# One 512-column matmul for the weights' high part instead of two of 256, with half-bank sums added on the way out, in a split-precision layer stack

## The chip, the core and the metric

The kernel runs on one core of a Trainium2 chip. The metric is the device time of one execution in microseconds. A profiled execution has a span of its own, from its first to its last instruction; TensorE (PE) multiplies, with its weight loads (PEld) beside it, VectorE (DVE) and ScalarE (ACT) do the element-wise work and are the engines that read the matmuls' results, GpSimd (POOL) does small powers and some transfers, and SyncE's queue issues most transfers.

## The reference

`x` is one sequence of 256 tokens with 1024 features. Two blocks follow one another, each two layers deep. The first block's layer is attention and an MLP, the second's is a gated feed-forward network, a mixer and another such network:

```
def hybrid_layer(x, ...):
    proj = rmsnorm(x, n1) @ w_in                    # 1024 -> 2304: two kinds of heads
    ...                                             # rope, global GQA, dilated window attention
    x = x + y @ w_out
    u = jnp.square(jax.nn.relu(rmsnorm(x, n2) @ w_mlp_in))    # 1024 -> 4096
    return x + u @ w_mlp_out

def second_block(x, ...):
    for l in range(DEPTH):
        f = swiglu(x, ffn_w_gate[l, 0], ffn_w_up[l, 0], ffn_w_down[l, 0])   # 1024 -> 2816 -> 1024
        x = layer_norm(ALPHA * x + 0.5 * f, ...)
        z = x @ w_in[l]                             # three mixers: spatial gating, short convolution, RG-LRU
        ...
        x = layer_norm(ALPHA * x + y @ w_out[l], ...)
        f = swiglu(x, ffn_w_gate[l, 1], ffn_w_up[l, 1], ffn_w_down[l, 1])
        x = layer_norm(ALPHA * x + 0.5 * f, ...)
```

All inputs and weights are float32.

## The kernel before

Every large product is done in a split precision. A float32 operand becomes a high part (its fp32r rounding) and a low part (what is left), and a product is three matmuls (`mm3`): high by high, high by low, low by high. Weights come in **units** of 256 columns (`in_unit`) or 256 rows (`out_unit`) of a matrix. A unit is loaded by two 512 KB transfers into `wraw`, ACT casts the high part into `whi`, DVE subtracts for the low part into `wlo` (line 153); four units fit, so units are made ready ahead of their use. The activations, transposed, lie in `xT`: a high tile `xh` and a low tile `xl`, 8 groups of 128 features by 256 tokens.

Three forms of product use them. `a_form` gives 128 tokens by 256 columns, with `xh` and `xl` as the stationary operand and the weights moving: 8 groups of features by 3 matmuls of 256 columns, 24 in all. `b_form` gives a transposed result of 256 columns by 256 tokens: for each half `f` of the unit's columns the weights are stationary and the 256 tokens of `xh` or `xl` move, 24 matmuls of 256 columns each, 48 for a unit; both halves fill one PSUM bank, and one instruction of ACT or DVE takes the whole bank out (Relu at line 584, Silu at 679, a multiplication at 688, a copy at 733). `out_form` multiplies a hidden unit by the rows of the down projection, with 512 columns moving, 24 matmuls for a unit (`out_both`).

PSUM is in three pools: four banks `acc`, two `rot` and two `aux`. `a_form`, attention values and half of the `b_form`s use `rot`; transposes (through `aux()`), the gates of the mixer and the other `b_form`s use `aux`.

The steady part of a feed-forward network alternates gate `b_form`, `out_both` of an older unit, up `b_form`. Between stages stands `enter`: the last sums of the old stage go token half by token half (`finish`), `norm(t)` normalizes a half of 128 tokens and transposes it into the new `xT` by two banks of four transposes (line 227 or 262), and `fn(t, i)` are the first four `a_form`s of the new stage:

```
        if finish is not None:
            finish(0)
            finish(1, [0])
            norm(0)
            finish(1, [1])
        fn(0, 0)
        norm(1)
        fn(0, 1)
        fn(1, 0)
        fn(1, 1)
```

In attention, a string gives the order of the work, "p2 h1 h0 h2 sa0 sa1 p5 ta0 p7 ...": `p` is a projection (two `a_form`s), `h` the transposes of its two token halves (line 355; a key half waits for the scale `kss`, line 335), `sa` scores (line 364), `ta` transposes of the softmax weights (line 399). The order in which instructions stand on each engine is made from such program order by a scheduler that may pull an instruction ahead of earlier ones. Each engine then works through its own instructions in the order fixed there.

Of the kernel before, what the change touches and what calls it, by code (L numbers as in the profile page):

```python
# [12 lines left out]
F32R = mybir.dt.float32r  # L13
# [6 lines left out]
P = 128  # L20
# [3 lines left out]
KT = 8  # L24
# [21 lines left out]
def hybrid_stack(ctx: ExitStack, tc: tile.TileContext, a, out):  # L46
# [11 lines left out]
    tmp = ctx.enter_context(tc.tile_pool(name="tmp", bufs=2))  # L58
    tiny = ctx.enter_context(tc.tile_pool(name="tiny", bufs=2))
    accp = ctx.enter_context(tc.tile_pool(name="accp", bufs=4, space=PSUM))  # L60
    rotp = ctx.enter_context(tc.tile_pool(name="rotp", bufs=2, space=PSUM))
    auxp = ctx.enter_context(tc.tile_pool(name="auxp", bufs=2, space=PSUM))

    uid = [0]

# [4 lines left out]
    def T(pool, shape, tag, dt=F32, **kw):  # L70
        return pool.tile(shape, dt, tag=tag, name=nm(tag), **kw)
# [13 lines left out]
    def pair(shape):  # L85
        return T(tmp, shape, "pair", bufs=2)
# [5 lines left out]
        return T(rotp, list(shape), "rot")  # L92

    def aux(shape=(P, 512)):
        return T(auxp, list(shape), "aux")

    def acc1(shape=(P, 512)):
        return T(accp, list(shape), "acc")
# [2 lines left out]
        return [[acc1() for _ in range(2)] for _ in range(NT)]  # L101

    def new_xT():
        return padded(xtp, [P, KT, S], "xh", F32R), padded(xtp, [P, KT, S], "xl", F32R)

    def chunks():
        return [(c, slice(c * 512, (c + 1) * 512)) for c in range(2)]
# [65 lines left out]
            mm3(o[:, :UN], xT[0][:, k, ts], xT[1][:, k, ts], w[k][0], w[k][1], k == 0, k == KT - 1)  # L173
        return o[:, :UN]

    def b_form(xT, w, o, between=None):
        o = o.rearrange("p (f s) -> p f s", f=2)
        for f in range(2):
            if f and between:
                between()  # L180
            for k in range(KT):
                fs = slice(f * P, (f + 1) * P)
                mm3(o[:, f], w[k][0][:, fs], w[k][1][:, fs], xT[0][:, k], xT[1][:, k], k == 0, k == KT - 1)
        return o

    def out_form(acc, hT, k0, w, t, c, first, last):
        ts = slice(t * P, (t + 1) * P)
# [389 lines left out]
    def mlp(l, xT, boundary):  # L577
        n = FF1 // UN
        w1, w2 = a["w_mlp_in"][l], a["w_mlp_out"][l]

        acted = []

        def act(ps, r):
            acted[:] = [se.activation(r, ps, AF.Relu), ve.tensor_tensor(r, r, r, op=ALU.mult)]
            return r

        na = 2
        ws = [in_unit(w1, u) for u in range(na)]
        hidden = {}

        def start(t, u):
            hidden[u, t] = act(a_form(xT, ws[u], t, rot()), T(tmp, [P, UN], "qk", bufs=9))

        enter(boundary, start)
        hts = []

        def first_T():
            hts.extend(new_hT() for _ in range(na))
            hidden_T(hts, hidden)

        acc = None
        last = []
        for u in range(n):
            if u + na < n:
                h = act(b_form(xT, in_unit(w1, u + na), (rot, aux)[u % 2](), None if u else first_T), pair([P, 2, S]))
                hT = new_hT()
                split(hT, slice(None), h)
                hts.append(hT)
            if u == 0:
                acc = new_acc()  # L610
            if l == 0 and u == n // 2:
                with behind(acted):
                    prepare()
            w = out_unit(w2, u)
            if u < n - 2:
                out_both(acc, hts[u], 0, w, u == 0)
            else:
                last.append((hts[u], 0, w))
        return acc, out_last(acc, last)
# [31 lines left out]
    def ffn(l, i, xT, boundary):  # L651
# [24 lines left out]
        for u in range(n):  # L676
            if u + 1 < n:
                h = pair([P, 2, S])
                se.activation(h, b_form(xT, in_unit(wg, u + 1), rot(), None if u else first_T), AF.Silu)
            if u == 0:  # L680
                acc = new_acc()
            w = out_unit(wd, u)
            if u < n - 2:
                out_both(acc, hts[u], 0, w, u == 0)
            else:
                last.append((hts[u], 0, w))
            if u + 1 < n:
                ve.tensor_tensor(h, b_form(xT, in_unit(wu, u + 1), aux()), h, op=ALU.mult)
                hT = new_hT()
                split(hT, slice(None), h)  # L690
                hts.append(hT)
        return acc, out_last(acc, last)

    def mixers(l, xT, boundary):
# [34 lines left out]
        bx = T(m4k, [P, 4, S], "m4k")  # L729

        def recur_in(u, c0):
            ps = b_form(xT, in_unit(w_in, u), rot())
            se.copy(xrp[:, c0:c0 + 2, 3:], ps)
            for c in range(c0, c0 + 2):
                se.activation(xc[:, c], xrp[:, c, 0:S], AF.Identity, scale=rw[:, 4 * c:4 * c + 1], bias=rb[:, c:c + 1])
                for k in range(1, 4):
                    ve.scalar_tensor_tensor(xc[:, c], xrp[:, c, k:k + S], rw[:, 4 * c + k:4 * c + k + 1], xc[:, c],
                                            ALU.mult, ALU.add)
# [29 lines left out]
        def short_conv():  # L768
# [1 line left out]
            cg = six([P, 2, S])  # L770
            cup = T(tmp, [P, 2, S + 2], "cup", bufs=1)
            gp.memset(cup[:, :, 0:2], 0.0)
            se.copy(bg, b_form(xT, in_unit(w_in, 2), rot()))
            se.copy(cg, b_form(xT, in_unit(w_in, 3), rot()))
            ps = b_form(xT, in_unit(w_in, 4), rot())
            ve.tensor_tensor(cup[:, :, 2:], ps, cg, op=ALU.mult)
            y = six([P, 2, S])
            for c in range(2):
                ve.tensor_scalar(y[:, c], cup[:, c, 0:S], sw[:, 3 * c:3 * c + 1], None, ALU.mult)
# [12 lines left out]
        gg = []  # L792
        for i in range(2):
            g = six([P, 2, S])
            last = se.activation(g, b_form(xT, in_unit(w_in, 5 + i), rot()), AF.Gelu_apprx_tanh)
            gg.append(g)
            transpose_to(yT, 0, i, uu[i], 2)
        aa = T(m4k, [P, 4, S], "m4k")
# [155 lines left out]
```

## Time and profile before

| | |
|---|---|
| time, median of 3 runs | 1549.0 us (1548.07 to 1549.47) |
| profiled execution: time | 1550.74 us |
| profiled execution: span | 1549.0 us |
| mean granted TensorE clock | 0.995 |
| TensorE matmuls | 1513.0 us busy, 98% of the span, 10480 instructions |
| TensorE weight loads | 1393.5 us, 10480 instructions |
| VectorE | 1014.4 us, 65% |
| ScalarE | 816.8 us, 53% |
| transfers | 272.98 MB, 176 GB/s on average |

A row gives the time an engine was busy and that time's share of the span. Matmuls are pipelined and their ends are modelled, so that a matmul's own duration is longer than the distance from its start to the next one's; the distances between starts tell the rate.

### The profile page before, as it was taken

How to read it: one execution, taken by the hardware profiler on the slowest of the kernel's cores; microseconds unless marked ns; L12 is line 12 of the kernel's file. 1: busy time of each engine (PE TensorE's matmuls, PEld its weight loads, DVE VectorE, ACT ScalarE, POOL GpSimd, SP SyncE). 2: the span in 40 equal slices, each digit the busy share in tenths (PEclk: the TensorE clock that was granted, in tenths of full speed). 3: DMA queues.
4: the chain of work that ended last, by engine and by line, in shares of the span. 5: the costliest groups of instructions: out<-in, count | busy, mean ns of one | idle time of the engine just before them, and what ended most of it. 6: DMA issues, size and time to landing. Idle time of an engine off the chain costs nothing. (4 is left out here: it accounts for less than half of the span.)

```text
span 1549.0 us, 27008 instructions
## 1 busy us (share of the span) xinstructions
PE 1513.0 (98%) x10480; PEld 1393.5 (90%) x10480; DVE 1014.4 (65%) x2044; ACT 816.8 (53%) x1636; POOL 77.9 (5%) x118
## 2 busy tenths in 40 slices
PE   7999999989999999999999999999999999999998
PEld 7889989889899898999989899999999989899997
DVE  7977556579775555655577875556755477875554
ACT  7766544478574545544446554443644446554441
POOL 4000000040000000000011000000000010000000
PEclk9999999999999999999999999999999999999999
DMA  6525655544356654766646476664766647476661
GB/s 216 173 63 167 217 189 183 173 113 154 111 190 190 191 179 146 237 191 188 189 141 205 158 227 184 190 189 136 246 190 190 191 128 219 150 239 185 188 186 47
DMA packets 196368, 272.98 MB, mean 176 GB/s; under 512 B 9312, under 2 KB 169600, under 8 KB 196240
## 3 DMA queue, kind: packets, MB, share of 16 engines
q1 hardware_dynamic: 193664, 262.76, 55.1%
q0 software_dynamic: 2576, 8.50, 1.8%
q8 instruction: 82, 1.34, 0.4%
q14 instruction: 46, 0.38, 0.1%
HBM read 270.17 MB, written 1.05 MB: 175 GB/s over the span
## 5 line engine op out<-in xcount | busy, mean ns | idle before, releaser
L153 DVE TENSOR_TENSOR wlo<-wraw,whi 128x512 fp32r<-128x512 f32 x992 | 640.7, 686 | 365.7 <-ACT whi L153 356.8
L153 ACT CAST whi<-wraw 128x512 fp32r<-128x512 f32 x992 | 565.1, 619 | 527.1 <-issue 262.0
L166 PE MATMUL rot<-xh,whi 128*128 128x256 f32 x1088 | 307.0, 282 | 0.0
L167 PE MATMUL rot<-xl,whi 128*128 128x256 f32 x1088 | 305.9, 281 | 0.0
L168 PE MATMUL rot<-xh,wlo 128*128 128x256 f32 x1088 | 305.9, 281 | 0.0
L167 PE MATMUL aux<-xl,whi 128*128 128x256 f32 x864 | 242.5, 281 | 0.0
L166 PE MATMUL aux<-xh,whi 128*128 128x256 f32 x864 | 242.1, 280 | 0.0
L168 PE MATMUL aux<-xh,wlo 128*128 128x256 f32 x864 | 242.1, 280 | 0.0
L166 PE MATMUL acc<-whi,six 128*128 128x512 f32 x608 | 240.7, 396 | 0.1
L168 PE MATMUL acc<-whi,six 128*128 128x512 f32 x608 | 239.2, 395 | 0.2
L167 PE MATMUL acc<-wlo,six 128*128 128x512 f32 x608 | 238.8, 393 | 0.0
L167 PEld LDWEIGHTS rot<-xl,whi 128*128 128x128 f32 x1088 | 205.2, 189 | 0.6
L166 PEld LDWEIGHTS rot<-xh,whi 128*128 128x128 f32 x1088 | 205.1, 188 | 0.7
L168 PEld LDWEIGHTS rot<-xh,wlo 128*128 128x128 f32 x1088 | 205.0, 188 | 0.2
L167 PEld LDWEIGHTS aux<-xl,whi 128*128 128x128 f32 x864 | 162.5, 188 | 2.3
L166 PEld LDWEIGHTS aux<-xh,whi 128*128 128x128 f32 x864 | 162.5, 188 | 2.2
L168 PEld LDWEIGHTS aux<-xh,wlo 128*128 128x128 f32 x864 | 162.5, 188 | 0.0
L168 PE MATMUL rot<-whi,xl 128*128 128x256 f32 x544 | 155.6, 288 | 2.7 <-DVE xl L222 2.6
L166 PE MATMUL rot<-whi,xh 128*128 128x256 f32 x544 | 157.2, 290 | 0.5 <-ACT qk L705 0.5
L167 PE MATMUL rot<-wlo,xh 128*128 128x256 f32 x544 | 155.7, 286 | 0.2 <-DVE wlo L153 0.2
L168 PEld LDWEIGHTS acc<-whi,six 128*128 128x128 f32 x608 | 114.1, 188 | 28.5 <-DVE six L222 1.6
L166 PEld LDWEIGHTS acc<-whi,six 128*128 128x128 f32 x608 | 114.3, 188 | 24.3 <-ACT six L221 1.8
(217 smaller groups left out, 1731.6 us busy)
## 6 DMA issues: line engine op xcount, KB each, us to landing
wraw<-in_ffn_w_gate_dram SPq DMA_DIRECT2D x88, 512.0 KB, 4.5
wraw<-in_ffn_w_up_dram SPq DMA_DIRECT2D x88, 512.0 KB, 4.4
wraw<-in_ffn_w_down_dram SPq DMA_DIRECT2D x88, 512.0 KB, 4.3
wraw<-in_w_in_dram SPq DMA_DIRECT2D x71, 512.0 KB, 4.6
wraw<-in_w_mlp_in_dram SPq DMA_DIRECT2D x64, 512.0 KB, 4.3
wraw<-in_w_mlp_out_dram SPq DMA_DIRECT2D x64, 512.0 KB, 4.1
wraw<-in_w_out_dram SPq DMA_DIRECT2D x32, 512.0 KB, 4.0
g<-in_ln_g_dram POOLq DMA_DIRECT2D x6, 512.0 KB, 3.8
```

Source lines behind the costliest of these rows:

```text
L153: done[:] = [se.copy(h, r), ve.tensor_tensor(l, r, h.bitcast(F32), op=ALU.subtract)]
L166: pe.matmul(o, lh, rh, start=first, stop=False)
L167: pe.matmul(o, lh, rl, start=False, stop=False)
L168: pe.matmul(o, ll, rh, start=False, stop=last)
```

## The change

`xh` and `xl` become the two halves of one tile, `xT`, of 512 columns for each group of features. In `b_form` one matmul of 512 columns, with the weights' high part stationary, meets both; a second one of 256 columns, with the weights' low part, meets the high half and adds to the left half of the bank. Each half `f` of the unit so fills a bank of its own, whose two halves have to be added: ACT copies the right half to SBUF, DVE adds the left half to it and writes the result to `dst`. What used to read PSUM now reads that result. `rot` and `aux` become one pool of four banks.

```
-    rotp = ctx.enter_context(tc.tile_pool(name="rotp", bufs=2, space=PSUM))
-    auxp = ctx.enter_context(tc.tile_pool(name="auxp", bufs=2, space=PSUM))
+    rotp = ctx.enter_context(tc.tile_pool(name="rotp", bufs=4, space=PSUM))
...
     def aux(shape=(P, 512)):
-        return T(auxp, list(shape), "aux")
+        return T(rotp, list(shape), "rot")
...
     def new_xT():
-        return padded(xtp, [P, KT, S], "xh", F32R), padded(xtp, [P, KT, S], "xl", F32R)
+        x2 = padded(xtp, [P, KT, 2 * S], "xT", F32R)
+        return x2[:, :, :S], x2[:, :, S:], x2
...
-    def b_form(xT, w, o, between=None):
-        o = o.rearrange("p (f s) -> p f s", f=2)
+    def b_form(xT, w, dst, between=None):
+        x2 = xT[2]
         for f in range(2):
             if f and between:
                 between()
+            fs = slice(f * P, (f + 1) * P)
+            o = rot()
             for k in range(KT):
-                fs = slice(f * P, (f + 1) * P)
-                mm3(o[:, f], w[k][0][:, fs], w[k][1][:, fs], xT[0][:, k], xT[1][:, k], k == 0, k == KT - 1)
-        return o
+                hi = lambda **kw: pe.matmul(o, w[k][0][:, fs], x2[:, k], **kw)
+                lo = lambda **kw: pe.matmul(o[:, :S], w[k][1][:, fs], x2[:, k, :S], **kw)
+                if k < KT - 1:
+                    hi(start=k == 0, stop=False)
+                    lo(start=False, stop=False)
+                else:
+                    lo(start=False, stop=False)
+                    hi(start=False, stop=True)
+            tb = T(tmp, [P, S], "ti", bufs=2)
+            se.copy(tb, o[:, S:])
+            ve.tensor_tensor(dst[:, f], o[:, :S], tb, op=ALU.add)
...
+        def square(r):
+            acted[:] = [ve.scalar_tensor_tensor(r, r, 0.0, r, ALU.max, ALU.mult)]
...
-                h = act(b_form(xT, in_unit(w1, u + na), (rot, aux)[u % 2](), None if u else first_T), pair([P, 2, S]))
+                h = pair([P, 2, S])
+                b_form(xT, in_unit(w1, u + na), h, None if u else first_T)
+                square(h)
...
-                se.activation(h, b_form(xT, in_unit(wg, u + 1), rot(), None if u else first_T), AF.Silu)
+                b_form(xT, in_unit(wg, u + 1), h, None if u else first_T)
+                se.activation(h, h, AF.Silu)
...
-                ve.tensor_tensor(h, b_form(xT, in_unit(wu, u + 1), aux()), h, op=ALU.mult)
+                up = four([P, 2, S])
+                b_form(xT, in_unit(wu, u + 1), up)
+                ve.tensor_tensor(h, up, h, op=ALU.mult)
...
-            ps = b_form(xT, in_unit(w_in, u), rot())
-            se.copy(xrp[:, c0:c0 + 2, 3:], ps)
+            b_form(xT, in_unit(w_in, u), xrp[:, c0:c0 + 2, 3:])
```

The other `b_form`s of the mixer change in the same way. Beyond these lines the change moves instructions that it does not touch, on PE at three places. The lines of the changed kernel are 12 to 20 higher than those of before (355 is 367 there, 364 is 376, 227 is 239, 743 is 762, 763 is 782).

The first is PE in attention of the first layer, behind projection p2. Before, the transposes of heads h1, h0 and h2 (line 355) stand between matmuls of projection p5 (`rot_605`):

```order
L355 MATMUL aux_525<-ident_99,qk_335 128x128 x2
L355 MATMUL aux_529<-ident_99,qk_413 128x128 x2
L166 MATMUL rot_605<-whi_590,xh_109 128x256
L167 MATMUL rot_605<-wlo_591,xh_109 128x256
L355 MATMUL aux_533<-ident_99,qk_260 128x128 x2
L168 MATMUL rot_605<-whi_590,xl_110 128x256
L355 MATMUL aux_537<-ident_99,qk_374 128x128 x2
L166 MATMUL rot_605<-whi_590,xh_109 128x256
...
L355 MATMUL aux_541<-ident_99,qk_477 128x128 x2
```

After `aux_541` (the first half of h2) 30 further matmuls of p5 stand ahead of the second half of h2, then 6 more and the scores. In the changed kernel all six stand together, ahead of p5 (`rot_600`), of which four matmuls stand ahead of the scores (line 376) and 44 behind them:

```order
L367 MATMUL rot_520<-ident_96,qk_330 128x128 x2
L367 MATMUL rot_524<-ident_96,qk_408 128x128 x2
L367 MATMUL rot_528<-ident_96,qk_255 128x128 x2
L367 MATMUL rot_532<-ident_96,qk_369 128x128 x2
L367 MATMUL rot_536<-ident_96,qk_472 128x128 x2
L367 MATMUL rot_540<-ident_96,qk_517 128x128 x2
L166 MATMUL rot_600<-whi_585,xT_106 128x256
L167 MATMUL rot_600<-wlo_586,xT_106 128x256
L168 MATMUL rot_600<-whi_585,xT_106 128x256
L166 MATMUL rot_600<-whi_585,xT_106 128x256
L376 MATMUL acc_544<-m4k_111,m4k_110 128x256
```

So p5 moved from between the transposes to behind the scores. The same holds in the second layer.

The second place is PE at `enter` in the second block, here from the first mixer to its feed-forward network. Before, the second token half's transposes (`x_7357`) stand behind the whole `a_form` of `fn(0, 0)`, 24 matmuls, and behind 19 of the 24 of `fn(0, 1)` (`rot_12405`):

```order
L227 MATMUL aux_12322<-ident_99,x_7291 128x128 x4
L227 MATMUL aux_12331<-ident_99,x_7291 128x128 x4
...
L166 MATMUL rot_12405<-whi_12267,xh_12240 128x256
L227 MATMUL aux_12389<-ident_99,x_7357 128x128 x4
L167 MATMUL rot_12405<-wlo_12268,xh_12240 128x256
L227 MATMUL aux_12398<-ident_99,x_7357 128x128 x4
L168 MATMUL rot_12405<-whi_12267,xl_12241 128x256
```

In the changed kernel (here from a network to the next) they stand ahead of all of `fn(0, 1)`, which is `rot_11704`:

```order
L239 MATMUL rot_11621<-ident_96,x_7001 128x128 x4
L239 MATMUL rot_11630<-ident_96,x_7001 128x128 x4
...
L168 MATMUL rot_11650<-whi_11550,xT_11540 128x256
L239 MATMUL rot_11688<-ident_96,x_7067 128x128 x4
L239 MATMUL rot_11697<-ident_96,x_7067 128x128 x4
L166 MATMUL rot_11704<-whi_11558,xT_11540 128x256
L167 MATMUL rot_11704<-wlo_11559,xT_11540 128x256
```

So 19 matmuls moved from ahead of these transposes to behind them. This is so at five boundaries: two into a mixer, two out of one, one between two networks. The other boundaries have the same order in both kernels.

The third is PE in the mixer, behind the sums of spatial gating (line 763). Before, the four gates (line 743) stand among the first 21 matmuls of the next `b_form` (`rot_9734`):

```order
L763 MATMUL aux_9662<-qk_9347,four_9491 128x64 x4
L763 MATMUL aux_9680<-qk_9429,four_9491 128x64 x4
L166 MATMUL rot_9734<-xh_9237,whi_9719 128x256
...
L743 MATMUL aux_9689<-m4k_9502,m4k_9496 128x256 x2
L168 MATMUL rot_9734<-xh_9237,wlo_9720 128x256
```

In the changed kernel the four stand together ahead of it:

```order
L782 MATMUL rot_9180<-qk_8886,four_9029 128x64 x4
L782 MATMUL rot_9198<-qk_8968,four_9029 128x64 x4
L762 MATMUL rot_9207<-m4k_9040,m4k_9034 128x256 x2
L762 MATMUL rot_9214<-m4k_9040,m4k_9034 128x256 x2
L762 MATMUL rot_9221<-m4k_9040,m4k_9034 128x256 x2
L762 MATMUL rot_9228<-m4k_9040,m4k_9034 128x256 x2
L186 MATMUL rot_9252<-xT_8777,whi_9237 128x512
```

So 21 matmuls moved behind the gates, in both layers.

## Rows read from the trace of the kernel before

**Rows 1.** The page: busy time of each engine, share of the span, instructions.
```profile
PE 1513.0 (98%) x10480; PEld 1393.5 (90%) x10480; DVE 1014.4 (65%) x2044; ACT 816.8 (53%) x1636; POOL 77.9 (5%) x118
```
**Rows 2.** Groups of TensorE: line, tiles, shape, count | busy us, mean ns | idle before.
```profile
L166 PE MATMUL rot<-xh,whi 128*128 128x256 f32 x1088 | 307.0, 282 | 0.0
...
L166 PE MATMUL aux<-xh,whi 128*128 128x256 f32 x864 | 242.1, 280 | 0.0
```
**Rows 3.** Timeline of PE in a feed-forward network: start us, duration us, operation.
```profile
666.20 0.39 PE L166 MATMUL acc<-whi,six 128*128 128x512 f32 x1
...
671.70 0.28 PE L166 MATMUL aux<-xh,whi 128*128 128x256 f32 x1
...
683.01 0.39 PE L166 MATMUL acc<-whi,six 128*128 128x512 f32 x1
...
688.56 0.28 PE L166 MATMUL aux<-xh,whi 128*128 128x256 f32 x1
```
**Rows 4.** Window of nearly nine feed-forward iterations: busy time (count) of PE, PEld, DVE, ACT.
```profile
640.00:790.00 150.00, 150.00 (x1090) 141.67 (x1089) 79.27 (x126) 70.00 (x126) 0.00 (x0) 1.00 0.64 192
```
**Rows 5.** Groups of ACT and of DVE that read a bank, or half of one.
```profile
L356 ACT COPY m4k<-aux 128x256 f32<-128x256 f32 x28 | 9.5, 375 | 6.1 <-PE aux L355 6.1
L584 ACT ACTIVATE pair<-rot 128x512 f32<-128x512 f32 x14 | 8.3, 595 | 0.0
L663 DVE TENSOR_TENSOR qk<-rot,qk 128x256 f32<-128x256 f32 x8 | 3.4, 419 | 0.3 <-PE rot L168 0.3
```
**Rows 6.** Timeline of PE in attention, first layer, with idle time and releaser.
```profile
40.75 0.41 PE L355 MATMUL aux<-ident,qk 128*128 128x128 f32 x2 [1.46 <-DVE qk L335]
...
41.79 2.00 PE L364 MATMUL acc<-m4k,m4k 64*128 64x256 f32 x16
...
49.77 0.44 PE L399 MATMUL aux<-ident,six 128*128 128x128 f32 x2 [2.12 <-DVE six L397]
```
**Rows 7.** The same, second layer.
```profile
340.76 0.41 PE L355 MATMUL aux<-ident,qk 128*128 128x128 f32 x2 [0.91 <-DVE qk L335]
...
348.83 0.44 PE L399 MATMUL aux<-ident,six 128*128 128x128 f32 x2 [1.15 <-DVE six L397]
```
**Rows 8.** Windows there; behind the five engines stands the granted clock.
```profile
336.00:338.00 2.00, 2.00 (x10) 2.00 (x11) 2.00 (x8) 1.34 (x4) 1.02 (x1) 0.50 0.24 19
338.00:341.00 3.00, 2.09 (x15) 1.92 (x14) 1.63 (x5) 1.06 (x3) 1.91 (x3) 0.83 0.74 218
```
**Rows 9.** Timeline at the first boundary out of a mixer: PE, then DVE.
```profile
887.48 1.25 PE L227 MATMUL aux<-ident,x 128*128 128x128 f32 x8
895.14 0.63 PE L227 MATMUL aux<-ident,x 128*128 128x128 f32 x4
...
889.38 1.28 DVE L222 TENSOR_TENSOR xl<-aux,xh 128x512 fp32r<-128x512 f32 x2
...
891.18 0.67 DVE L290 SCALAR_TENSOR_TENSOR x<-acc,x 128x512 f32<-128x512 f32 x1
894.25 1.41 DVE L299 SCALAR_TENSOR_TENSOR x<-x,lms,b 128x512 f32<-128x512 f32 x2
```
**Rows 10.** Timeline of PE at the first boundary into a mixer.
```profile
809.76 0.38 PE L166 MATMUL rot<-whi,xh 128*128 128x256 f32 x1 [0.26 <-ACT qk L705]
...
811.56 0.39 PE L168 MATMUL rot<-whi,xl 128*128 128x256 f32 x1 [1.30 <-DVE xl L222]
```
**Rows 11.** Timeline of PE at the gates, first and second mixer.
```profile
828.18 1.89 PE L763 MATMUL aux<-qk,four 128*128 128x64 f32 x16
...
839.86 0.47 PE L166 MATMUL rot<-xh,whi 128*128 128x256 f32 x1
...
1295.29 1.89 PE L763 MATMUL aux<-qk,four 128*128 128x64 f32 x16
1301.55 1.89 PE L743 MATMUL aux<-m4k,m4k 128*128 128x256 f32 x8
1303.09 0.47 PE L166 MATMUL rot<-xh,whi 128*128 128x256 f32 x1
```

More of the change, by code (lines that the diff above doesn't have):

```diff
@@ L772, in short_conv @@
             gp.memset(cup[:, :, 0:2], 0.0)
[L773 to L776, printed above, removed]
+            b_form(xT, in_unit(w_in, 2), bg)
+            b_form(xT, in_unit(w_in, 3), cg)
+            b_form(xT, in_unit(w_in, 4), cup[:, :, 2:])
+            ve.tensor_tensor(cup[:, :, 2:], cup[:, :, 2:], cg, op=ALU.mult)
             y = six([P, 2, S])
@@ L794, in mixers @@
             g = six([P, 2, S])
-            last = se.activation(g, b_form(xT, in_unit(w_in, 5 + i), rot()), AF.Gelu_apprx_tanh)
+            b_form(xT, in_unit(w_in, 5 + i), g)
+            last = se.activation(g, g, AF.Gelu_apprx_tanh)
             gg.append(g)
```

## The prediction

> **What bounds the kernel now.** I read the page first: matmuls are busy for 98% of the span, DVE for 65%, ACT for 53% [rows 1]. So the question is where TensorE (PE) stands still, and what a matmul costs it. The groups show that `b_form`'s matmuls have no idle time before them [rows 2]: where they run, PE alone sets the pace. Its idle time lies at a few places that the timeline shows: attention, where transposes wait for DVE [rows 6, 7], the boundary into a mixer [rows 10] and the gates [rows 11]. The windows show that in a steady feed-forward stretch DVE works 79 and ACT 70 of 150 us [rows 4]: they wait for PE, not PE for them. The change can therefore gain only by making PE's own stream shorter, and lose by making PE wait where it does not wait now.
>
> **The steps of the matmuls.** `b_form` has 1088 + 864 = 1952 groups of three matmuls [rows 2]. From 671.70 to 683.01 there are two `b_form`s, 96 matmuls of 256 columns: 11.31 / 96 = 117.8 ns from start to start. From 683.01 to 688.56 stand 24 matmuls of 512 columns: 5.55 / 24 = 231.3 ns; from 666.20 to 671.70 another 24 take 5.50, 229.2 ns [rows 3]. A group costs 3 x 117.8 = 353.4 ns before, and 231.3 + 117.8 = 349.1 after, if the new 512-column matmul, whose moving operand is the activation, runs like these, whose moving operand is the weight. That is 4.3 ns for each group, **-8 us** in all (1952 x 4.3 ns = 8.4). The bounds are the columns alone (768 before and after: no gain, 0 us) and the shorter stretch (6.4 ns, -12 us). So nearly all that PE streams stays; the third weight load that goes lay beside a matmul.
>
> The Trainium skill (TensorE: Matmul & The Clock Gate, Back-to-back issue gap) gives the distance of matmuls at the full clock as the columns at 2.4 GHz plus 2.5 ns. By it each group saves 2.5 ns, 4.9 us in all, and the sum below would end 3 us higher; but it would also make the steps 109 and 216 ns, where this trace shows 118 and 231 [rows 3], so the rows decide.
>
> **The way out.** Each of the 122 `b_form`s (1952 / 16) gets two ACT copies and two DVE additions of 128x256. The nearest rows are 375 ns for an ACT copy out of a bank and 419 ns for a DVE operation with one operand in PSUM [rows 5]: 244 x 0.375 = 92 us on ACT, 244 x 0.419 = 102 us on DVE. Against this the MLP's 28 Relus of 595 ns go from ACT [rows 5]; its squares stay one DVE instruction, and Silu and the product read SBUF instead of PSUM. In 150 us stand about 8.9 iterations of 16.8 us, with 4 of each: DVE goes from 79 to about 94 us, ACT from 70 to about 83 [rows 4]. The cover is PE's own work: a hidden unit is used only after another `b_form` of 5.65 us [rows 3], and the added chain is below 1 us. I take 0. With that cover gone it would be 122 x 0.8 = 98 us, if each wait stood open on PE.
>
> **Attention.** Here p5 moves behind the scores. In the first layer the second half of head h2 is transposed at 40.75, released by DVE, after PE had idled 1.46 us; the chain of `kss` through DVE and POOL keeps its place in both orders, so this time stays [rows 6]. Before, PE has run 42 matmuls of p5 by then and spends the stretch from the scores (41.79, 2.00 us) to the first `ta0` transposes (49.77) on 31 of p7 and 2.12 us of waiting [rows 6]. After, it waits without cover ahead of 40.75, and then has p5's 44 matmuls, 44 x 0.118 = 5.2 us, for the same gap; they end near 49. At 49.77 PE has saved at most 0.9 us of `ta0` against 31 x 0.118 = 3.7 us of p7 not yet done: 2.8 us late. In the second layer 16 matmuls of p7 stand ahead of `ta0` at 348.83 [rows 7]: 16 x 0.118 = 1.9 us late. Nothing behind it gives this back, for PE has little idle time there.
>
> The clock adds to it. In the second layer, after PE had waited, the granted clock was 0.50 from 336 to 338 and still 0.83 on average to 341 [rows 8]: half of 2.4 GHz for 2 us and, at 0.83 of a mean, for (1 - 0.83) x 2 x 3 = 1.0 us more, 3 us at the least. Before, part of that spell lay where PE waited anyway. After, PE has hardly any work for 8 us ahead of the scores in both layers, and the spell falls on p5 and the scores: 3 / 2 = 1.5 us each. The bounds are 0 and twice that. Attention: 2.8 + 1.9 + 2 x 1.5 = **+7.7 us**.
>
> **Boundaries.** At 887.48 the first token half is transposed, at 895.14 the second, 7.66 us later [rows 9]. What lies between on DVE is a chain that the change leaves in its order: `xl` at 889.38, statistics, the sum at 891.18, the last normalization from 894.25, and the transposes stand right behind it [rows 9]. PE filled this with 8 transposes, 6 matmuls of 512 and 43 of 256 columns. Now 19 of the 43 stand behind the transposes, so PE comes 19 x 0.118 = 2.2 us early and waits; behind the transposes they cover nothing, since PE does not wait there now. Three boundaries (two out of a mixer, one between networks): 3 x 2.2 = 6.6 us. At the two into a mixer PE waits behind the transposes now, 0.26 + 1.30 us [rows 10], and the 19 matmuls cover that: 2 x (2.2 - 1.6) = 1.2 us. **+7.8 us.** The bounds are 0, if DVE's chain came 2.2 us sooner, and 11. A fall of the clock behind each wait (1.5 us, five times) is left to the range.
>
> **Gates.** From the gating sums to the end of the gates and 21 matmuls PE takes 11.68 us in the first mixer and 7.80 in the second, of which 1.89 + 4 x 0.77 + 21 x 0.118 = 7.45 is work (two gates from 1301.55 to 1303.09) [rows 11]. The gates wait for DVE and ACT in the first. With the 21 matmuls behind them, up to 2.5 us of cover goes; against that each half of a projection's channels now leaves PSUM 2.8 us before the other, which brings the inputs sooner. The bounds are 0 and 5; I take **+1 us**.
>
> **Sum:** -8 + 7.7 + 7.8 + 1 = +8.5 us. Against the profiled execution, 1550.7 us with a span of 1549.0, that gives 1559.2; its time lies 1.7 us above the median, so the median goes from 1549.0 to 1557.5, **1558 us**.
>
> **Rivals.**
> 1. *About even, 1549 us.* The waits are shorter than the matmuls that left them, because DVE or ACT reach the chains sooner with four shared banks: half of attention and of the boundaries, 8 instead of 15.5, cancels the 8 us. For it: a bank no longer waits for its one partner. Against it: the chains end in DVE and POOL [rows 6, 9], which no bank holds up.
> 2. *Faster, 1541 us.* The saving of 8 us comes alone. The mechanism is the place of PE's late releases: DVE's normalization of the second half would have to end 2.2 us sooner than at 895, and the `kss` chain some 3 us sooner than at 40.75; from half of that on it gains. The rows show both chains busy without gaps that the change could take out.
> 3. *Slower by more, 1565 us.* The clock falls at each of the five boundaries, 5 x 1.5 = 7.5 us. For it: it fell behind waits of this length in attention [rows 8]. Against it: the mean granted clock of the whole span is 0.995, so of PE's many waits few end in a fall.
> 4. *Evacuation binds, above 1580 us.* The additions hold up DVE's subtractions for the weights, which stand behind them in its queue, and PE waits for `wlo`. It decides where DVE has under 15 us of 150 to spare; it has 70 [rows 4].
>
> **How the numbers follow.** My case has 0.64 and its own range is 1552 to 1565; rival 1 has 0.15, rival 2 0.10, rival 3 0.08, rival 4 0.03. The runs of before lie within 0.1% of each other, so 0.2%, 3.1 us, is about what a measurement can tell from no change. Slower by more than that: my case but for its lowest edge, and rivals 3 and 4, 0.74. Within it: rival 1 and that edge, 0.16. Faster: 0.10. The range takes in the upper half of rival 1 and rival 3 up to its time: 1547 to 1566.
>
> **What would show it.** In the changed profile the matmuls and weight loads should be 8528 each (10480 - 1952); 512-column steps in `b_form` of 229 to 235 ns and 256-column ones near 118; PE idle for 3 to 5 us ahead of each key head's second half, with the clock at 0.5 behind it; a wait of about 2 us released by DVE ahead of the second transposes at five boundaries; DVE near 1115 us and ACT near 890, without PE waiting for either in the networks. I am wrong if `b_form` groups fall below 340 ns, if DVE's chain ends sooner at the boundaries, or if PE waits inside the networks.

## The result, and the profile after

The changed kernel takes 1570.0 us (median of 4 runs, 1567.6 to 1572.4) against 1548.5 beside it: a ratio of 1.0137, 95% interval 1.0122 to 1.0152. It is slower, as forecast, but by 21.5 us where 8.5 were worked out, and 4 us above the range. The profiled execution has a span of 1570.6 us.

The page of the changed kernel, the line of [rows 1], and two of its groups, which answer to [rows 2]:

```profile
PE 1514.8 (96%) x8528; PEld 1305.4 (83%) x8528; DVE 1113.9 (71%) x2288; ACT 879.3 (56%) x1844; POOL 79.0 (5%) x118
L186 PE MATMUL rot<-xT,whi 128*128 128x512 f32 x1952 | 681.8, 396 | 0.0
L187 PE MATMUL rot<-xT,wlo 128*128 128x256 f32 x1952 | 507.1, 280 | 0.0
```

The counts came as worked out (8528), the two engines' busy times nearly so (1115 and 890 us were given), and nothing stands idle ahead of a `b_form`. So what the loss is made of lies elsewhere, and a table by stage says where. A stage is counted from its first normalized transposes (line 262 or 227, 274 or 239 after) to those of the next, as the timelines show them; the last ends with the last matmul.

| stage | before, us | after | difference |
|---|---|---|---|
| attention, first layer | 121.40 | 128.68 | +7.28 |
| MLP | 182.03 | 181.83 | -0.20 |
| attention, second layer | 118.22 | 122.03 | +3.81 |
| MLP | 182.92 | 182.18 | -0.74 |
| network | 190.94 | 191.17 | +0.23 |
| mixer | 87.67 | 86.99 | -0.68 |
| network | 189.07 | 192.45 | +3.37 |
| network | 188.88 | 192.84 | +3.96 |
| mixer | 85.05 | 88.83 | +3.78 |
| network | 190.84 | 192.02 | +1.18 |

With -0.34 us at the start that is +21.65. Attention has half of it, although it holds no `b_form` at all. These are stages of one profiled execution of each kernel; how much the first one varies while its order stays is said further below.

**Steps of the matmuls.** The timeline of the changed kernel where two `b_form`s follow one another, as in [rows 3]:

```profile
664.35 0.40 PE L186 MATMUL rot<-xT,whi 128*128 128x512 f32 x1
...
675.63 0.40 PE L166 MATMUL acc<-whi,six 128*128 128x512 f32 x1
```

675.63 - 664.35 = 11.28 us for 32 groups, against 11.31 in [rows 3]. Over the 34 such pairs of each trace the mean went from 11.325 to 11.246 us: 2.5 ns a group, 4.8 us in all instead of 8.4. The new 512-column matmul stands 233.6 ns ahead of the next start (the mean over the trace, without steps over 270 ns), not 231.3. By the gap formula of the Trainium skill (TensorE: Matmul & The Clock Gate, Back-to-back issue gap), which the page gives for an isolated matmul, the saving is estimated at 2.5 ns a group, as measured, though the formula's steps of 109 and 216 ns stand in neither trace.

**Attention.** TensorE in the first layer after the change, to be read beside [rows 6], and the windows of the half-speed stretches in both layers (behind the five engines stands the granted clock):

```profile
36.95 0.66 PE L367 MATMUL rot<-ident,qk 128*128 128x128 f32 x2 [4.53 <-DVE qk L347]
42.35 0.66 PE L367 MATMUL rot<-ident,qk 128*128 128x128 f32 x2 [4.74 <-DVE qk L347]
43.80 2.98 PE L376 MATMUL acc<-m4k,m4k 64*128 64x256 f32 x16
52.09 1.03 PE L411 MATMUL rot<-ident,six 128*128 128x128 f32 x8
```
```profile
38.00:46.00 8.00, 3.65 (x18) 3.08 (x20) 6.63 (x18) 4.74 (x10) 2.94 (x3) 0.51 0.70 192
343.00:353.00 10.00, 5.83 (x25) 4.09 (x24) 7.34 (x20) 5.40 (x11) 2.93 (x3) 0.50 0.66 198
```

TensorE waits ahead of both halves of the key head, 4.5 and 4.7 us. Before, the second of these waits was 1.46 [rows 6], and the first:

```profile
35.35 0.41 PE L355 MATMUL aux<-ident,qk 128*128 128x128 f32 x2 [1.68 <-DVE qk L335]
```

The clock goes to half for 10.24 us in each layer, and for 3.41 us at 103.9 in the first, where the kernel before has one such fall, 3.41 us long, in the second; the scores take 2.98 instead of 2.00 us; and the `ta0` transposes come 2.3 us later than in [rows 6], at 52.09, when all of p5 but none of p7 is done.

**Boundaries.** At the first boundary out of a mixer, which [rows 9] show for before: TensorE, then DVE and ACT ahead of it.

```profile
896.83 1.29 PE L239 MATMUL rot<-ident,x 128*128 128x128 f32 x8 [1.97 <-DVE x L311]
904.53 1.29 PE L239 MATMUL rot<-ident,x 128*128 128x128 f32 x8 [2.14 <-DVE x L311]
...
888.10 1.29 DVE L153 TENSOR_TENSOR wlo<-wraw,whi 128x512 fp32r<-128x512 f32 x2 [0.84 <-ACT whi L153]
890.33 1.29 DVE L153 TENSOR_TENSOR wlo<-wraw,whi 128x512 fp32r<-128x512 f32 x2 [0.93 <-ACT whi L153]
891.54 0.68 DVE L302 SCALAR_TENSOR_TENSOR x<-acc,x 128x512 f32<-128x512 f32 x1
...
889.67 1.15 ACT L153 CAST whi<-wraw 128x512 fp32r<-128x512 f32 x2 [1.09 <-DMA wraw<-in_ffn_w_up_dram]
```

The wait ahead of the second transposes is the 2.2 us that was forecast. The one ahead of the first, 1.97 us here and as long behind the second mixer, was not: DVE comes to the sum `x<-acc` only when it has done ten subtractions for the next network's weights, and the last two wait for a cast of ACT, which waits for a transfer. Before, seven subtractions stand directly ahead of the same sum, and it waits for its matmuls alone:

```profile
880.75 0.69 DVE L290 SCALAR_TENSOR_TENSOR x<-acc,x 128x512 f32<-128x512 f32 x1 [0.31 <-PE acc L168]
```

**Gates.** From the gating sums to the end of the gates and 21 matmuls' worth of `b_form` (7 groups of 0.35 us), the stretch of [rows 11]:

```profile
839.57 1.89 PE L782 MATMUL rot<-qk,four 128*128 128x64 f32 x16
...
845.53 0.59 PE L186 MATMUL rot<-xT,whi 128*128 128x512 f32 x1
...
1310.69 1.89 PE L782 MATMUL rot<-qk,four 128*128 128x64 f32 x16
...
1319.52 0.58 PE L186 MATMUL rot<-xT,whi 128*128 128x512 f32 x1
```

845.53 + 2.46 - 839.57 = 8.4 us in the first mixer, 11.3 in the second, against 11.68 and 7.80: -3.3 in the one and +3.5 in the other, +0.2 us in all.

### The profile page after: what moved, and what is told of

Read it like the earlier page. It is cut to its first block, busy times and chain, and to the rows that moved or that the text cites. A ratio compares the mean times of both kernels' runs of the same rounds, so it can differ in the third digit from the quotient of the medians.

```text
span 1570.6 us, 23644 instructions
## 1 busy us (share of the span) xinstructions
PE 1514.8 (96%) x8528; PEld 1305.4 (83%) x8528; DVE 1113.9 (71%) x2288; ACT 879.3 (56%) x1844; POOL 79.0 (5%) x118
## 5 line engine op out<-in xcount | busy, mean ns | idle before, releaser
L186 PE MATMUL rot<-xT,whi 128*128 128x512 f32 x1952 | 681.8, 396 | 0.0
L187 PE MATMUL rot<-xT,wlo 128*128 128x256 f32 x1952 | 507.1, 280 | 0.0
L186 PEld LDWEIGHTS rot<-xT,whi 128*128 128x128 f32 x1952 | 355.4, 188 | 68.9
L187 PEld LDWEIGHTS rot<-xT,wlo 128*128 128x128 f32 x1952 | 367.2, 188 | 21.5
L195 ACT COPY ti<-rot 128x256 f32<-128x256 f32 x244 | 90.9, 372 | 162.0 <-PE rot L186 162.0
L166 PE MATMUL rot<-whi,xT 128*128 128x256 f32 x544 | 158.4, 292 | 2.8 <-ACT whi L153 2.8
L168 PE MATMUL rot<-whi,xT 128*128 128x256 f32 x544 | 155.8, 287 | 1.6 <-DVE xT L234 1.6
L167 PE MATMUL rot<-wlo,xT 128*128 128x256 f32 x544 | 156.5, 288 | 0.1
L167 PEld LDWEIGHTS acc<-wlo,six 128*128 128x128 f32 x608 | 114.1, 188 | 26.2
L166 PEld LDWEIGHTS rot<-whi,xT 128*128 128x128 f32 x544 | 106.5, 196 | 3.9 <-ACT whi L153 3.2
L167 PEld LDWEIGHTS rot<-wlo,xT 128*128 128x128 f32 x544 | 106.4, 195 | 2.3 <-issue 1.0
L168 PEld LDWEIGHTS rot<-whi,xT 128*128 128x128 f32 x544 | 105.8, 195 | 2.2 <-DVE xT L234 2.2
```

The source lines that it names most:

```text
L166: pe.matmul(o, lh, rh, start=first, stop=False)
L167: pe.matmul(o, lh, rl, start=False, stop=False)
L168: pe.matmul(o, ll, rh, start=False, stop=last)
L186: hi = lambda **kw: pe.matmul(o, w[k][0][:, fs], x2[:, k], **kw)
L187: lo = lambda **kw: pe.matmul(o[:, :S], w[k][1][:, fs], x2[:, k, :S], **kw)
L195: se.copy(tb, o[:, S:])
```

## The experiments

The theory after the result was that nothing but the order costs time, and that the order comes from the common pool: a tile of a pool is not given out ahead of one that was asked for earlier, so with one pool p5's bank stands behind the head's banks in line. The orders below agree with that rule of giving out banks; no run tests the rule by itself. Two edits that the change makes together were therefore taken apart.

**One pool alone.** In the kernel before:

```
-    rotp = ... tile_pool(name="rotp", bufs=2, space=PSUM)
-    auxp = ... tile_pool(name="auxp", bufs=2, space=PSUM)
+    rotp = ... tile_pool(name="rotp", bufs=4, space=PSUM)
```

> The kernel before, with its rot and aux banks in one pool of four and nothing else changed; its instructions stand in the order of the changed kernel in attention, at the boundaries and at the gates. Theory A (the common pool's order is the loss, the matmul form is a gain of 5.3 us): 1548.5 + 21.5 + 5.3 = 1575 us, with PE waiting 4 to 5 us at each key head and 2.2 us ahead of the second transposes. Theory B (the additions on the way out delay DVE's chains at the boundaries, 4.4 us of the loss in the trace): 1571 us, without the 2.1 us waits ahead of the first transposes out of a mixer. Theory C (the 512-column form itself is the loss): 1549 us.

1571.9 us, ratio 1.0146 (1.0132 to 1.0159): the pool alone costs as much as the whole change. Its stages of attention take 128.52 and 121.68 us, as in the changed kernel. Theory C is out. At the boundary out of the first mixer:

```profile
895.93 1.29 PE L226 MATMUL rot<-ident,x 128*128 128x128 f32 x8
903.64 1.29 PE L226 MATMUL rot<-ident,x 128*128 128x128 f32 x8 [2.15 <-DVE x L298]
```

There is a wait ahead of the second transposes, none ahead of the first, so that one needs the new `b_form` as well, as theory B has it.

**Two pools, a half of each `b_form` in either.** In the changed kernel, the pools of before, and:

```
-            o = rot()
+            o = (rot, aux)[f]()
```

> The changed kernel with two pools of two banks again; half 0 of each b_form takes a rot bank, half 1 an aux bank. The order of before comes back. Theory A: the saving of the steps alone, 1548.5 - 5.3 = 1543 us. Theory B: 1548 us, since the additions stay in DVE's queue ahead of the normalizations. Theory C: 1570 us as the changed kernel.

1560.1 us, ratio 1.0073 (1.0060 to 1.0085): none of the three. Attention came back to 123.42 and 120.22 us, but each MLP and network has a new wait in its first `b_form`:

```profile
148.63 0.51 PE L167 MATMUL acc<-whi,six 128*128 128x512 f32 x1 [1.12 <-ACT six L234]
```

The second half takes an aux bank, the hidden unit's transposes hold aux banks, and so the order put matmuls of `out_both` between the halves, which wait for those transposes. Six such waits are 7.2 us; the 8.3 us named further below count short ones in the mixers too. The run also keeps the waits ahead of the first transposes (2.07 and 1.94 us), with ten subtractions ahead of the sum in DVE's queue as in the changed kernel.

**p5 ahead of h2 in the string**, one pool:

```
-    "p2 h1 h0 h2 sa0 sa1 p5 ta0 p7 ...
+    "p2 h1 h0 p5 h2 sa0 sa1 ta0 p7 ...
```

> The changed kernel with its one pool, and projection p5 ahead of head h2 in the string of attention, which is all that changes. Theory A (PE idles at the key heads because no matmuls are left to stand there, and the clock falls behind that): both layers get back what they lost, 7.3 + 3.8 = 11 us, 1559 us. Rival (only the waits come back, the wait moves behind the scores and the clock falls all the same): 1566 us. Rival (the chain of kss sets the pace wherever p5 stands): 1570 us.

1574.6 us, ratio 1.0170 (1.0154 to 1.0186), outside all three. The timeline of the second layer:

```profile
345.53 3.78 PE L376 MATMUL acc<-m4k,m4k 64*128 64x256 f32 x16 [0.65 <-ACT m4k L368]
354.11 3.17 PE L376 MATMUL acc<-m4k,m4k 64*128 64x256 f32 x8 [4.79 <-ACT six L395]
```

With p5 gone from there, the third scores were pulled up behind the second, where they wait 4.79 us for a softmax to give back a bank of `acc`. In the first layer the two waits at the key head did shrink to one of 2.36 us, and the layer took 125.20 us for 128.68; the second took 129.54 for 122.03. A string in this kernel is a wish, and its place on TensorE has to be read afterwards; the time of this run says nothing for or against the theory.

**Second transposes behind all of fn(0, 1)**, one pool, at every boundary:

```
         fn(0, 0)
-        norm(1)
         fn(0, 1)
+        norm(1)
```

> The changed kernel with its one pool, and at every boundary the second token half's normalization and transposes behind all of fn(0, 1), 24 matmuls of 256 columns. Theory A (the transposes stand 2.3 us too early in PE's queue at five boundaries and the clock falls behind two of them): 5 x 2.3 + 3.4 less 1 to 4 us of new waits behind the transposes, 1558 to 1560 us. Theory B (DVE's chain ends late because of the additions, whatever stands on PE): PE waits for the products that follow instead, 1567 us.

1564.5 us, ratio 1.0098 (1.0084 to 1.0111), 5.5 us less than the changed kernel, between the two. At the boundary of the rows above:

```profile
902.91 1.03 PE L239 MATMUL rot<-ident,x 128*128 128x128 f32 x8
904.18 0.38 PE L166 MATMUL rot<-whi,xT 128*128 128x256 f32 x1 [0.24 <-ACT xT L233]
905.33 0.38 PE L168 MATMUL rot<-whi,xT 128*128 128x256 f32 x1 [0.42 <-DVE xT L234]
```

The wait ahead of the second transposes is gone, and 0.66 us came back behind them, where nothing covers ACT's and DVE's work on what was transposed. At the two boundaries into a mixer it is 1.8 and 1.9 us, more than the theory had allowed.

**Two pools, both halves in rot.** The changed kernel with the pools of before and nothing else:

> Two pools of two banks again, and both halves of every b_form take rot banks; the order on PE is that of before nearly everywhere. Theory D (in the run with halves in both pools, 8.3 us were waits of the first b_form of a stage for an aux bank that its transposes held; what is left is 4 us of waiting ahead of the first transposes behind the two mixers, some 3.5 us of clock falls, and -5.3 us of steps): 1560.1 - 8.3 = 1552 us. Rival, the additions are not hidden at the start of a stage, whatever bank they read: 1560 us. Theory A as it stood: 1543 us.

1545.9 us, ratio 0.9986 (0.9977 to 0.9995): this version beats both kernels, by 0.14% and 1.5%. It is between theories A and D; the 4 us ahead of the first transposes that D kept are not there. Its DVE, at the end of the first mixer:

```profile
876.63 4.90 DVE L154 TENSOR_TENSOR wlo<-wraw,whi 128x512 fp32r<-128x512 f32 x8
881.45 0.68 DVE L303 SCALAR_TENSOR_TENSOR x<-acc,x 128x512 f32<-128x512 f32 x1
```

Eight subtractions stand ahead of the sum, not ten. The additions of the mixer are all still there, so they do not bring the wait by themselves, as theory B had it. The wait goes with how far the weights' work was pulled ahead in DVE's queue: seven subtractions directly ahead of the sum in the kernel before and with the pool alone, eight here, and no such wait; ten in the changed kernel and in the run with a half in either pool, and a wait behind both mixers.

**The same, with the mixers' b_forms as before** (three matmuls, one read of the bank, at the seven units of a mixer):

> As the run with two pools and all halves in rot, but the mixers' b_forms are again three matmuls of 256 columns with one read of the bank; networks and MLP keep the 512-column form. Theory D (the mixer's additions on DVE wait for PE and hold up the weights' subtractions behind them, so that the normalization at the mixer's end starts late): the 4 us ahead of the first transposes go, 14 x 16 x 2.7 ns = 0.6 us of steps come back, 1548.5 us. Rival, the normalization is late because the weights' transfers are late: 1552 us, with the waits still there.

1546.8 us, ratio 0.9988 (0.9979 to 0.9997), no different from the run above. With nothing waiting there any more, the run could not tell its theories apart; what it shows is that the new form costs the mixers nothing that can be measured.

**The way out twice**, one pool:

```
+            for _ in range(2 if twice else 1):
-            se.copy(tb, o[:, S:])
-            ve.tensor_tensor(dst[:, f], o[:, :S], tb, op=ALU.add)
+                se.copy(tb, o[:, S:])
+                ve.tensor_tensor(dst[:, f], o[:, :S], tb, op=ALU.add)
```

> The changed kernel with one pool, and in the networks and the MLP each copy of ACT and each addition of DVE on the way out is done twice (108 b_forms, 216 copies and 216 additions more: 80 us more on ACT, 91 on DVE). If the way out lies beside PE's work there: 1570 us as the changed kernel, within 3 us. Rival, it stands on the path at the start and the end of each stage (12 places by 2 x 0.8 us): 1580 us or more. If it stood open everywhere: 1656 us.

1571.1 us, ratio 1.0143 (1.0129 to 1.0157), 1.1 us above the changed kernel and within its runs. The windows of a steady stretch, the changed kernel and this one (PE, PEld, DVE, ACT):

```profile
640.00:790.00 150.00, 149.98 (x785) 127.31 (x784) 95.95 (x166) 84.67 (x168) 0.54 (x1) 1.00 0.65 198
```
```profile
640.00:790.00 150.00, 150.00 (x785) 127.64 (x786) 108.64 (x201) 94.22 (x201) 0.54 (x1) 1.00 0.65 196
```

DVE and ACT take on 13 and 10 us more in 150, and TensorE does not stop. The way out is hidden. The doubled one shows at the ends of networks: there are waits of 1.65, 1.22 and 1.66 us ahead of the first transposes at three boundaries where the changed kernel has none, and most of that comes back, since the wait ahead of the second transposes is 0.8 us shorter at two of them and gone at the third.

**p5 behind the scores**, in the version with two pools. This gives attention the changed kernel's order without its pool:

```
         def proj(u):
             w = in_unit(w_in, u)
-            for t in range(NT):
-                post[u](a_form(xT, w, t, rot()), t)
+            with behind(scored if u == 5 else []):
+                for t in range(NT):
+                    post[u](a_form(xT, w, t, rot()), t)
```

(`scored` is the last matmul of the scores; `behind` queues on its engine only.)

> The run with two pools and all halves in rot (1545.9 us), with the matmuls of projection p5 queued behind the scores on TensorE, as they stand in the changed kernel; boundaries and gates stay as they were. Theory (the order in attention, not the pool itself, costs the changed kernel 7.3 and 3.8 us there): both attention layers take about what they take in the changed kernel, 128.7 and 122.0 us, so 1545.9 + 4 + 4 = 1554 us (its first layer already held two clock falls). Rival (the common pool costs banks, not order): no change, 1546 us.

1555.7 us, ratio 1.0048 (1.0031 to 1.0065), 9.7 us above the version it starts from (8 were forecast); attention takes 129.59 and 124.29 us in the profiled execution, the slowest of the five with 1560.7 us.

```profile
36.52 0.66 PE L369 MATMUL aux<-ident,qk 128*128 128x128 f32 x2 [4.25 <-DVE qk L349]
41.91 0.66 PE L369 MATMUL aux<-ident,qk 128*128 128x128 f32 x2 [4.73 <-DVE qk L349]
43.03 3.65 PE L378 MATMUL acc<-m4k,m4k 64*128 64x256 f32 x16 [0.46 <-ACT m4k L370]
```

The waits are those of the changed kernel, with the banks of before. In attention the order is the cause, and the pool only by way of it.

**The waits filled.** The changed kernel, one pool, with 36 matmuls that nobody reads ahead of each half of the key head:

```
             for t in range(NT):
+                if u == 2 and t in (0, 1):
+                    o = rot()
+                    for i in range(36):
+                        pe.matmul(o[:, :S], xT[0][:, 0, :P], xT[0][:, i % KT], start=i == 0, stop=i == 35)
                 heads_T(*dest[u], t, held.pop((u, t)))
```

> The changed kernel, with 36 matmuls of 256 columns, whose result nobody reads, ahead of each token half's transposes of the key head in attention: 4.2 us of work in each of the four waits of 4.3 to 5.1 us. Theory (half of what attention loses is the clock that falls behind the waits, 10.24 us at half in each layer): the falls there go, 2 x 10.24 / 2 = 10 us at most, 1560 to 1563 us. Rival (the fall costs nothing more, since the chain through DVE and GpSimd sets the pace): 1570 us. Rival (the added work comes late and costs its own length where the wait was shorter): above 1572 us.

1570.6 us, ratio 1.0145 (1.0131 to 1.0159), as the changed kernel. TensorE, then ACT, in the first layer:

```profile
36.97 4.55 PE L519 MATMUL rot<-xT 128*128 128x256 f32 x36
42.20 0.41 PE L367 MATMUL rot<-ident,qk 128*128 128x128 f32 x2 [0.69 <-DVE qk L347]
45.32 3.48 PE L376 MATMUL acc<-m4k,m4k 64*128 64x256 f32 x16 [2.23 <-ACT m4k L368]
...
43.85 1.14 ACT L153 CAST whi<-wraw 128x512 fp32r<-128x512 f32 x2 [1.10 <-DMA wraw<-in_w_in_dram]
44.90 0.36 ACT L368 COPY m4k<-rot 128x256 f32<-128x256 f32 x1
```

The half-speed stretches shrank from 10.24 to 3.41 us in each layer, but the scores start later, at 45.32 instead of 43.80: the copy of the key head now stands in ACT's queue behind a cast that waits for a transfer. What the clock alone costs in attention stays open.

**Two of GpSimd's three operations on DVE**, in the version with two pools:

```
-        gp.tensor_scalar(rq, rq, rx[:, 2:3], EPS, ALU.mult, ALU.add)
+        ve.tensor_scalar(rq, rq, rx[:, 2:3], EPS, ALU.mult, ALU.add)
         gp.tensor_tensor(rq, rq, nhalf[:, :nh], op=ALU.pow)
-        gp.tensor_scalar(rq, rq, rx[:, 0:1], None, ALU.mult)
+        ve.tensor_scalar(rq, rq, rx[:, 0:1], None, ALU.mult)
```

> The run with two pools and all halves in rot, with two of GpSimd's three operations for each query and key scale (a multiplication ahead of the power and one behind it) on DVE. Theory (GpSimd's small operations take up to 2.9 us there while DVE works on 512 columns, 0.3 us where DVE is idle, and the scores wait for that chain): the waits ahead of the key head's transposes get shorter by 2 to 4 us in each layer, 1540 to 1543 us. Rival (each change of engine costs what the operation saves, or DVE's own queue makes it wait): 1546 us or more.

1548.2 us, ratio 0.9995 (0.9985 to 1.0006): no gain over 1545.9, as the rival said. GpSimd's part shrank to the power, but the power starts no sooner, at 36.61 and 40.89 against 34.76 and 40.16, because DVE's queue puts weights and waits for the query scales ahead of the key:

```profile
36.61 0.74 POOL L331 TENSOR_TENSOR kss<-kss,nhalf 128x2 f32<-128x2 f32 x1 [5.37 <-DVE kss L330]
40.89 0.74 POOL L331 TENSOR_TENSOR kss<-kss,nhalf 128x2 f32<-128x2 f32 x1 [3.54 <-DVE kss L330]
```

**The up projection's first unit later**, one pool: in `ffn`, `in_unit(wu, 0)` moves from ahead of `enter` to the first use.

> The changed kernel, with the up projection's first unit made ready behind the first normalization of a feed-forward network instead of ahead of it: at the end of a mixer 6 instead of 10 subtractions for weights stand ahead of the first sum x<-acc in DVE's queue. Theory (DVE waits there for a transfer by way of ACT's cast, which makes the first normalization 2.1 and 2.3 us late in the changed kernel): those two waits go, 4.4 us and perhaps a clock fall, 1564 to 1566 us. Rival (the normalization waits for the matmuls' sums anyway): 1570 us. Rival (the unit comes late where it is used): above 1572 us.

1573.5 us, ratio 1.0157 (1.0142 to 1.0173). Both halves of it came true: DVE's sum waits only for its matmuls, and the two mixers take 84.43 and 85.22 us instead of 86.99 and 88.83, without a wait ahead of the first transposes; but the unit is late where it is used, in every network. DVE, then TensorE:

```profile
883.50 3.69 DVE L153 TENSOR_TENSOR wlo<-wraw,whi 128x512 fp32r<-128x512 f32 x6
887.92 0.69 DVE L302 SCALAR_TENSOR_TENSOR x<-acc,x 128x512 f32<-128x512 f32 x1 [0.72 <-PE acc L168]
...
904.80 0.77 PE L166 MATMUL rot<-whi,xT 128*128 128x256 f32 x2 [1.19 <-ACT whi L153]
```

So the subtractions for a late transfer, ahead in DVE's queue, are what makes the first normalization late, and this is not the way to mend it.

## Why the prediction was right or wrong

The direction and the mechanism were right: the matmuls give little, the way out is hidden, and the moved instructions cost more. The size was wrong, and the step that failed is that DVE's work at a boundary is "a chain that the change leaves in its order". At the ends of both mixers ten subtractions stand ahead of the sum instead of seven, and TensorE waits 4.4 us for it. Term by term, on the profiled executions:

| term | forecast, us | measured |
|---|---|---|
| steps of the matmuls | -8 | -4.8 |
| way out | 0 | 0 (1.1 for twice of it) |
| attention | +7.7 | +11.1 |
| boundaries, second transposes | +7.8 | +9.9 |
| boundaries, first transposes | not there | +4.4 |
| gates | +1 | +0.2 |
| what is left, clock falls at the boundaries included | falls left to the range | 0.9, by subtraction |
| sum | +8.5 | +21.7 |

*Steps.* The condition was "if the new 512-column matmul, whose moving operand is the activation, runs like these, whose moving operand is the weight". It stands 233.6 ns ahead of the next start, not 231.3, so the gain was 2.5 ns a group.

*Attention.* A step that did not hold is "the chain of `kss` through DVE and POOL keeps its place in both orders, so this time stays". In the first layer the second half of the head came at 42.35 instead of 40.75. GpSimd's multiplications ahead of that chain, of before and of the changed kernel:

```profile
28.10 0.79 POOL L319 TENSOR_SCALAR rqA<-rqA,rms 128x4 f32<-128x4 f32 x1
28.98 1.08 POOL L317 TENSOR_SCALAR rqA<-rqA,rms 128x4 f32<-128x4 f32 x1
31.59 1.52 POOL L319 TENSOR_SCALAR rqA<-rqA,rms 128x4 f32<-128x4 f32 x1
```
```profile
28.22 2.86 POOL L331 TENSOR_SCALAR rqA<-rqA,rms 128x4 f32<-128x4 f32 x1
31.16 2.03 POOL L329 TENSOR_SCALAR rqA<-rqA,rms 128x4 f32<-128x4 f32 x1
34.41 0.30 POOL L331 TENSOR_SCALAR rqA<-rqA,rms 128x4 f32<-128x4 f32 x1
```

The first two of these instructions, with the same order ahead of them, take 3.0 us longer here; the third gives part of it back, and the chain ends 1.6 us later (34.71 for 33.11). Of the runs with attention's order of before, two show the long pattern (the two with two pools and the new form throughout) and one the short (the one with the mixers' old form). With the changed order the pool alone shows the long one, the doubled way out and the later weights the short one. So these 1.6 us are not the change's, and the profiled execution had them by chance. At an equal pattern the first layer loses about 5 us: 126.5 and 127.2 against 121.4 and 121.8 in the short one, 128.7 and 128.5 against 124.5 and 123.4 in the long one. 2.8 + 1.5 = 4.3 was worked out. What is left is size: the scores themselves fell into the half-speed stretch (2.98 us for 2.00), and `ta0` came 2.3 us later, not 0.9 earlier. In the second layer 3.4 us were worked out and 3.8 measured.

*Boundaries.* The wait of "about 2 us released by DVE ahead of the second transposes at five boundaries" stands there five times, 2.3 us each. What failed is "a chain that the change leaves in its order": that was read on TensorE and on DVE from the first transposes on. Ahead of them, at the ends of both mixers, subtractions for a late transfer had moved in front of the sum, and 2.13 + 2.28 us of waiting with them (each the distance of two starts less a matmul of 232 ns). The term of the second transposes is the five waits, 11.57 us, and 2.08 behind the first transposes, 13.65 us, against 3.71 behind the second ones before.

*Gates.* They came near the forecast by luck: -3.3 us in the first mixer and +3.5 in the second, where +1 had been taken for both together.

*Clock.* It fell four times in the second block, against twice before; one of each lies at the gates. A fall at a boundary does cost time. From the second transposes to the first `b_form`, out of the first mixer with a fall and out of the second without, these are the same 80 matmuls (the clock is the third number from the end):

```profile
904.53:915.66 11.13, 11.09 (x80) 10.88 (x81) 8.92 (x15) 6.97 (x14) 0.63 (x2) 0.85 0.70 200
1378.65:1388.23 9.58, 9.54 (x80) 9.34 (x81) 7.84 (x14) 6.59 (x13) 0.59 (x2) 1.00 0.74 223
```

That is 1.55 us, the 1.5 that the prediction had left to its range. Three falls against one would be some 3 us, more than the 0.9 that is left in the table, so some 2 us came back elsewhere, and where is not shown.

*The rivals.* Rival 1, shorter waits, did not come: the waits are 2.3 us each. Rival 3 (a fall at each of the five boundaries, 1565) came nearest in size, with falls at three of them. Rival 4 is shown false by the doubled way out. Rival 2, the saving alone, needs the order to stay, and the version with two pools, in which it stays, takes 1545.9; outside attention its stages are 5.4 us shorter than before in sum. 3.4 of that are in the first mixer, where this execution has no clock fall and 0.4 instead of 2.3 us of waiting at the gates, so about 2 us at most are the steps.

What stays open: what the half-speed stretches cost in attention by themselves, why GpSimd falls into one pattern or the other, and why no more than 2 of the 4.8 us of the steps show in that version's stages.

## What to carry to other kernels

A pool is part of the program's order: merging two pools of banks left a pair of `b_form`s at 11.325 us and still cost 23 us, because work that used to fill a wait was no longer pulled ahead of it. Change the arithmetic and the pools in separate steps, and after each read the order on every engine that feeds a wait, DVE's queue as much as TensorE's. Two matmuls in place of three, with the same columns, were worth 2.5 ns of 354 here.

## What was not expected of the hardware

GpSimd's multiplication of 128x4 took 0.30 us at 34.41, while DVE stood idle and waited for what follows it, and 2.86 us at 28.22, while DVE worked without a pause, 1.9 us of it on three subtractions of 128x512 with both operands in SBUF. The Trainium skill (SBUF — State Buffer, SBUF: two separate sides) has a rule for it: a DVE operation with two SBUF inputs and a GpSimd operation that reads SBUF hold their common ports in turn, each for its whole length. The rows do not settle it: beside the same operations of DVE, in the same order, the kernel before took 0.79 us, and one subtraction takes no more than 0.69. No run here takes the subtractions away, so the cause is argued only. And the clock stayed at half for 10.24 us behind the two waits of attention, where each fall of the kernel before lasted 3.41 us.
